# A hybrid attention and state-space block on one core: the last unit's sums of one head on VectorE, w_out split earlier, and the gates' loads and buffers

## The chip, the cores and the metric

The kernel runs on one core of a Trainium2 chip. Its engines work side by side, each through a queue of its own in the order of that queue: TensorE (PE in the profile, its weight loads PEld), VectorE (DVE), ScalarE (ACT), GpSimd (POOL) and SyncE (SP), which here only issues transfers. The metric is the device time of one execution in microseconds; lower is better.

## The reference

One layer of a hybrid encoder: a normalised input is projected once and feeds attention and a state-space layer, whose gated and normalised outputs are joined and projected.

```python
xn = rmsnorm(h, pre_norm_w)                       # h: 16 meta tokens + 2048 tokens, width 1024
proj = einsum('bld,de->ble', xn, w_in)
q_lat, kv_lat, k_rope, attn_gate, ssm_u, ssm_gate = split(proj, ...)
...                                               # q, k (64 + 32 rotary) and v for 8 heads
y_attn = block_attention(qf, kf, vf)              # softmax(q k / sqrt(96)) v, bidirectional
y_attn = rmsnorm(y_attn * silu(attn_gate), attn_out_norm_w)
...
y_ssm = s5(forward) + s5(backward) + ssm_d * ssm_u
y_ssm = glu(gelu(y_ssm))                          # w_glu, b_glu
y_ssm = rmsnorm(y_ssm * silu(ssm_gate), ssm_out_norm_w)
y = einsum('bld,de->ble', concat([y_attn, y_ssm]), w_out)
return (h + rmsnorm(y, post_norm_w))[:, 16:]
```

All is float32. The kernel gets the precision from three matmuls of rounded parts: high x high, high x low, low x high.

## The kernel before, in words

**A planner sets each engine's order.** The kernel's parts are Python generators (streams). A planner keeps a modelled clock for each engine, lets each stream name what it needs next (`Need`: data, an engine, PSUM banks, a condition), and issues the stream that could start first, then by rank. A stream with a due time waits behind the others until the attention's `progress` has reached it; `progress` is the number of the unit plus the share of it that is issued. So the order on each engine is fixed when the program is built. Every engine call goes through one helper, so all rows of the profile show line L190, and the names of the tiles tell them apart.

**Gates.** For 8 blocks of 256 tokens, `gates` multiplies the tokens (`x2h`, `x2l`, loaded by `gates_prep` from `xt_d` in four transfers a block) with the gates' weights, in 8 groups `m` of 48 matmuls `pg`. ACT copies each result into a buffer `gs`, of which there are three, and SP writes it to `gate_d`. Beside it runs the state-space layer: PE's `z` matmuls need `mbt`, an ACT copy, and `md` tables come in eight transfers a group on SP's queue.

**Attention.** 16 units (4 pairs of heads by 4 blocks of 512 queries). `b_main` takes 17 key tiles `t` by two heads `h`: three `sc` matmuls on PE, the exponential `pp` on ACT (12 buffers), and a sum over the key tiles, `acc[h]`, for the softmax's denominator, one add a tile from `t` = 1 on, on POOL. In the last unit, 15, the two adds of `t` = 15 and the two of `t` = 16 go to DVE. `b_pv` follows with the `pv` matmuls in groups of three or four tiles. After each unit, `finish` adds up `acc` over the partitions (`sm` on PE, a copy `sms` on ACT), takes reciprocals in four pieces on DVE, sends them through memory and scales the unit's output `ot` with it and with the gate `gt` on POOL.

**Preparation of the output projection.** `glu_main` ends with the split of w_out: 8 slices of 128 rows, two halves each, with two ACT operations (`ws_o` into a PSUM bank, the cast `wo`) and a subtraction on DVE (`wo`, `wo_l`) for each half; after the last, POOL scales the post-norm weights, `pw`. Only then the streams `c_stat` and `c_split` are added. `c_stat` squares a block of 256 tokens on ACT (`sq_c`), adds it up on DVE and over the partitions on PE (`pss`); `c_split` splits the tokens into high and low (`yy`, ACT and DVE). Block 0 needs only the attention's units up to 12.

**Tail.** `c_late` does the output projection, `po`, in 24 matmuls a segment of 512 columns, for 16 tiles of 128 tokens, and `c_post` the post-norm and the residual.

Of the kernel before, what the change touches and what calls it, by code (L numbers as in the profile page):

```python
# [11 lines left out]
F32 = mybir.dt.float32  # L12
# [3 lines left out]
ALU = mybir.AluOpType  # L16
# [4 lines left out]
P = 128  # L21
D = 1024
EPS = 1e-6
NJ = 16
# [243 lines left out]
def body(ctx: ExitStack, tc: tile.TileContext, x, meta_tokens, pre_norm_w, post_norm_w, w_in,  # L268
# [5 lines left out]
    V, A, PE, POOL, SP = (Engine(clock, n, e) for n, e in (  # L274
        ("V", nc.vector), ("A", nc.scalar), ("PE", nc.tensor), ("P", nc.gpsimd), ("SP", nc.sync)))
# [57 lines left out]
    pools, stacks, floors = {}, {}, {"left": 0.0, "right": 0.0}  # L333
# [8 lines left out]
    def close_pool(name):  # L342
        st, side = stacks.pop(name)
        st.close()
        pools.pop(name)
        floors[side] = max([clock.last(t) for t, h in clock.home.items() if h[0] == name] + [floors[side]])

    psum = Pool(clock, "psum", ctx.enter_context(tc.tile_pool(name="psum", bufs=1, space=PSUM)), 0.0)
    banks = {"a": (0, 1), "b": (2, 3), "c": (4, 5), "d": (6,), "e": (7,), "de": (6, 7),
             "sc": (0, 1, 5), "sc3": (0, 1, 5, 4), "pm": (2, 3, 6), "pm0": (6, 7, 1), "k0": (4, 5), "g": (2, 3, 0), "y": (7, 1), "gl": (4,)}  # L350
# [5 lines left out]
    def pst(use, name, shape=(P, 512)):  # L356

        k = next_bank(use)
        turns[use] += 1
        return psum.tile(shape, F32, tag=f"ps_{k}", name=name)  # L360
# [11 lines left out]
    done = {}  # L372
# [218 lines left out]
    def split(hi, lo, src, scale=None):  # L591

        if scale is None:
            A.copy(hi, src)
            V.tensor_tensor(lo, src, hi.bitcast(F32), ALU.subtract)
        else:
            A.activation(hi, src, AF.Copy, scale=scale)
            V.scalar_tensor_tensor(lo, src, scale, hi.bitcast(F32), ALU.mult, ALU.subtract)
# [14 lines left out]
    def pair(p):  # L613

        return ((slice(0, 2), (0, 1)), (slice(0, 3, 2), (1, 0)), (slice(1, 3), (0, 1)))[p % 3]
# [482 lines left out]
    def gates_prep():  # L1098
        xg = pools["xg"]
        st["rrow2"] = xg.tile([P, 2, P], F32, name="rrow2")  # L1100
        SP.dma_start(st["rrow2"].rearrange("p t c -> p (t c)"),
                     rx_d.rearrange("t c -> (t c)").unsqueeze(0).broadcast_to([P, 256]))
        gx[7] = tuple(x3[h].rearrange("p s k c -> p k s c")[:, :, pair(7)[0]] for h in "hl")
        for n, b in enumerate(GO):
            if n == 0:
                continue
            yield Need(when=lambda n=n: done.get("gate", 0) >= n - 1)
            xx = [(xg if n % 2 else xp).tile([P, 8, 2, P], F32R, tag="x" + h, name="x2" + h) for h in "hl"]
            for t in range(2):
                for x_ in range(2):  # L1110
                    SP.dma_start(xx[x_][:, :, t].bitcast(F32), xt_d[2 * b + t, x_])
            gx[b] = xx
            done["gx"] = n

    def gates():
        for b in GO:
            yield Need(when=lambda b=b: b in gx)
            xh, xl = gx.pop(b)
            for m in range(8):
                yield Need(banks=["g"])  # L1120
                pg = pst("g", "pg", (P, 2, P))
                for k in range(8):
                    if k % 2 == 0:
                        yield Need(when=lambda k=k: done.get("wg", 0) >= k + 2)
                        yield Need(st["wg_l"][k], st["wg_l"][k + 1], xl[:, k], xl[:, k + 1])
                    for i, (xx, ww) in enumerate(((xh, "wg_h"), (xh, "wg_l"), (xl, "wg_h"))):
                        PE.matmul(pg, st[ww][k][:, m * P:(m + 1) * P], xx[:, k],
                                  start=(k == 0 and i == 0), stop=(k == 7 and i == 2))
                gs = pools["xg"].tile([P, 2, P], F32, tag="gs", name="gs", bufs=3)
                if b == 0:  # L1130

                    yield Need(pg, st["rrow2"])
                    V.tensor_tensor(gs, pg, st["rrow2"], ALU.mult)
                elif b < 7:
                    A.copy(gs, pg)
                else:
                    for t_, t in enumerate(pair(7)[1]):
                        A.copy(gs[:, t], pg[:, t_])
                SP.dma_start(gate_d[m, :, b * 256:(b + 1) * 256], gs.rearrange("p t c -> p (t c)"))
            done["gate"] = done.get("gate", 0) + 1  # L1140
        close_pool("xg")
        close_pool("xp")
        close_pool("wt")
        order.add(b_open2(), -2)
# [326 lines left out]
    def b_open2():  # L1471

        yield Need(when=lambda: "kp" in pools)
        open_pool("bst", "right")
        open_pool("gl", "right")
        b_load_v(0)
        order.add(b_main(), 0)
        order.add(b_pv(), 0.2)
        order.add(b_gate(), -2.5)
        order.add(glu_main(), -0.5)  # L1480

    def b_load_v(p):
        vp = pools["bst"].tile([P, 17, P], F32, tag="vp", name="vp", bufs=2)
        SP.dma_start(vp[:, 0:NJ], v_d[0:NJ, :, p * P:(p + 1) * P].rearrange("j c e -> c j e"))
        SP.dma_start(vp[:16, NJ], v_d[NJ, :16, p * P:(p + 1) * P])
        vps[p] = vp
# [135 lines left out]
    def b_main():  # L1622
        bs = pools["bst"]
        for u in range(16):
            p, qb = divmod(u, 4)
            b = p % 2
            yield Need(when=lambda u=u: u in qts)
            if qb == 1 and p < 3:
                b_load_v(p + 1)
            qh, ql = qts.pop(u)  # L1630
            yield Need(when=lambda u=u: done.get("fin", 0) >= u - 1)
            acc = [bs.tile([P, 512], F32, tag=f"acc{h}", name=f"acc{h}", bufs=2) for h in range(2)]
            accs[u], first = acc, []
            for t in range(17):
                n = P if t < NJ else 16
                ks = slice(t * P, t * P + n)
                for h in range(2):

                    bk = "sc3" if "glu" in done else "sc"
                    yield Need(qh[h], banks=[bk],  # L1640
                               when=lambda k=(2 * (17 * u + t) + h - PPB) // 2: done.get("pv", 0) > k)
                    sc = pst(bk, "sc")
                    PE.matmul(sc[:n], kh[b, h][:, ks], qh[h], start=True, stop=False)
                    PE.matmul(sc[:n], kl[b, h][:, ks], qh[h][0:96], start=False, stop=False)
                    PE.matmul(sc[:n], kh[b, h][0:96, ks], ql[h], start=False, stop=True)
                    pp = bs.tile([P, 512], F32, tag="pp", name="pp", bufs=PPB)
                    A.activation(pp[:n], sc[:n], AF.Exp, scale=SCALE)
                    if t == 1:
                        POOL.tensor_tensor(acc[h], first[h], pp, ALU.add)
                    elif t > 1:  # L1650
                        (V if u == 15 and t >= NJ - 1 else POOL).tensor_tensor(acc[h][:n], acc[h][:n], pp[:n], ALU.add)
                    if t == 0:
                        first.append(pp)
                    pps.setdefault((u, t), []).append(pp)
                    order.progress = u + (t + 0.5 * h + 0.5) / 17
            done["unit"] = u + 1
            clock.lat = 2.2
# [28 lines left out]
    def glu_main():  # L1686
# [3 lines left out]
        for k in range(4):  # L1690
            raw = gl.tile([P, D], F32, tag="ysv", name="rawl", bufs=2)
# [8 lines left out]
        for b in range(8):  # L1700
# [30 lines left out]
            for m in range(4):  # L1731
                for half_ in range(2):
                    mm = m + 4 * half_
                    for k in range(4):
                        if k % 2 == 0:
                            yield Need(gl_, banks=["gl"] if (half_, k) == (0, 0) else [],
                                       due=d0 + (mm_ + 1) * 1.2 / 18)
# [21 lines left out]
        for k in range(8):  # L1759
            raw = pools["kp"].tile([P, D], F32, tag="k00" + "01"[k % 2], name="rawo")  # L1760
            SP.dma_start(raw, w_out[k * P:(k + 1) * P, :])
            if k == 7:

                yield Need(when=lambda: "q15" in done)
                st["wo"][1].append(pools["qp"].tile([P, D], F32R, tag="q4", name="wo_l7", bufs=1))
            for hv in range(2):
                c = slice(hv * 512, hv * 512 + 512)
                yield Need(raw, eng="A V", banks=["pm"], due=12.6 + k * 0.36 + hv * 0.18)
                ws = pst("pm", "ws_o")
                A.activation(ws, raw[:, c], AF.Copy, scale=cols[:, AOW + k:AOW + k + 1])  # L1770
                split(st["wo"][0][k][:, c], st["wo"][1][k][:, c], ws)
# [221 lines left out]
```

## Time and profile before

| what | us |
| --- | --- |
| median of 3 runs | 1697.39 (1694.19 to 1698.38) |
| profiled execution, its own time | 1692.8 |
| its span in the profile | 1691.0 |
| mean granted clock of PE in it | 0.99 of full speed |

The span is what the profiler saw from the first to the last instruction; the time of the same execution is 1.8 us more. Of the span, PE is busy nearly all, and the slices of the page in which it is not are few. The start times of rows count from the span's start: PE's last `pv` of unit 15 ends at about 1479, and the tail follows.

### The profile page before, as it was taken

What the parts mean: (1) busy time and instruction counts of PE and PEld (TensorE: products, weight loads), DVE (VectorE), ACT (ScalarE), POOL (GpSimd) and SP (SyncE); (2) the same over time, 40 slices, a digit from 0 to 9 for tenths busy, and PEclk for the clock granted to TensorE, in tenths of its full rate; (3) what the DMA queues carried; (4) which work ended last, traced back from release to release, by engine and by line L of the source; (5) the groups of instructions that cost most, each with busy time, mean ns of one, the idle gap of its engine ahead of it and who ended that gap; (6) DMA issues with size and microseconds to landing.
All of it is one profiled execution on the core that took longest, in us unless ns stands there. A gap on an engine that the chain in (4) does not pass through costs nothing. (4 is left out here: it accounts for less than half of the span.)

```text
span 1691.0 us, 28589 instructions
## 1 busy us (share of the span) xinstructions
PE 1641.0 (97%) x10320; PEld 1278.0 (76%) x10320; DVE 1082.2 (64%) x2543; ACT 781.4 (46%) x1628; POOL 805.8 (48%) x686
## 2 busy tenths in 40 slices
PE   8999999999989999999999999999999999979998
PEld 7897999999989966667767676767676666557776
DVE  5688634899987466665556557555745556157775
ACT  4543334435535246444444545354544555534433
POOL 0010012000000157877787778787878999922222
PEclk9999999999999999999999999999999999989999
DMA  9865645463445652112111202121111011123431
GB/s 221 267 209 145 208 141 174 125 176 117 143 135 166 157 151 86 41 57 66 42 59 40 75 25 63 54 70 36 45 41 59 27 60 58 64 92 138 150 125 50
DMA packets 179539, 175.68 MB, mean 104 GB/s; under 512 B 35419, under 2 KB 153110, under 8 KB 178118
## 3 DMA queue, kind: packets, MB, share of 16 engines
q1 hardware_dynamic: 179382, 173.86, 33.7%
q8 instruction: 81, 1.33, 0.3%
q14 instruction: 60, 0.49, 0.1%
q10 hardware_dynamic: 16, 0.00, 0.0%
HBM read 110.28 MB, written 63.54 MB: 103 GB/s over the span
## 5 line engine op out<-in xcount | busy, mean ns | idle before, releaser
L190 POOL TENSOR_TENSOR acc<-acc,pp 128x512 f32<-128x512 f32 (+1 forms) x476 | 595.2, 1283 | 87.4 <-ACT pp L190 86.9
L190 ACT ACTIVATE pp<-sc 128x512 f32<-128x512 f32 (+1 forms) x544 | 320.1, 598 | 319.5 <-PE sc L190 303.3
L190 DVE TENSOR_REDUCE mx<-pm 128x1 f32<-128x412 f32 (+1 forms) x640 | 340.3, 580 | 129.0 <-PE pm L190 126.8
L190 PE MATMUL sc<-qh,kh 97*128 97x512 f32 (+1 forms) x544 | 220.7, 406 | 1.8 <-DVE qh L190 1.8
L190 PE MATMUL sc<-qh,kl 96*128 96x512 f32 (+1 forms) x544 | 217.0, 399 | 0.0
L190 PE MATMUL sc<-ql,kh 96*128 96x512 f32 (+1 forms) x544 | 215.3, 396 | 0.0
L190 PE MATMUL pm<-kh,qh 96*128 96x412 f32 (+1 forms) x640 | 187.9, 359 | 0.6 <-ACT qh L190 0.2
L190 PE MATMUL po<-wo,yy 128*128 128x512 f32 (+1 forms) x759 | 181.5, 393 | 0.1
L190 PEld LDWEIGHTS po<-wo,yy 128*128 128x128 f32 x759 | 140.6, 190 | 34.4 <-ACT rps L190 1.2
L190 PEld LDWEIGHTS pm<-kh,qh 96*128 96x128 f32 x640 | 115.8, 188 | 55.2 <-issue 18.6
L190 PE MATMUL pg<-x2h,wg_h 128*128 128x256 f32 x448 | 130.4, 291 | 0.0
L190 PEld LDWEIGHTS sc<-qh,kh 97*128 97x128 f32 (+1 forms) x544 | 100.0, 184 | 38.5 <-issue 20.2
L190 PE MATMUL pg<-x2h,wg_l 128*128 128x256 f32 x448 | 126.7, 283 | 0.0
L190 PE MATMUL pg<-x2l,wg_h 128*128 128x256 f32 x448 | 126.6, 283 | 0.0
L190 PEld LDWEIGHTS sc<-ql,kh 96*128 96x128 f32 (+1 forms) x544 | 101.0, 186 | 27.2
L190 POOL TENSOR_TENSOR ta<-qs,cs 128x512 f32<-128x512 f32 x8 | 10.9, 1365 | 221.9 <-ACT qs L190 136.3
L190 POOL TENSOR_TENSOR t_c<-o_c,pw 128x512 f32<-128x512 f32 (+1 forms) x33 | 41.9, 1269 | 145.4 <-DVE o_c L190 124.6
L190 PEld LDWEIGHTS sc<-qh,kl 96*128 96x128 f32 (+1 forms) x544 | 101.1, 186 | 10.8
L190 POOL COPY U<-um 128x4 f32<-128x4 f32 x16 | 5.5, 349 | 214.9 <-issue 147.4
L190 PE MATMUL pa_c<-gh,wl 128*128 128x256 f32 x512 | 103.8, 284 | 0.6 <-DVE gl__13652 L190 0.6
L190 PEld LDWEIGHTS pa_c<-gh,wl 128*128 128x128 f32 x512 | 84.0, 190 | 6.3 <-issue 2.5
L190 PEld LDWEIGHTS pg<-x2h,wg_h 128*128 128x128 f32 x448 | 85.7, 191 | 1.4 <-issue 1.2
(458 smaller groups left out, 3344.8 us busy)
## 6 DMA issues: line engine op xcount, KB each, us to landing
raw<-in_x_dram SPq DMA_DIRECT2D x16, 512.0 KB
gate_d<-gs SPq DMA_DIRECT2D x64, 128.0 KB
md<-g_d SPq DMA_DIRECT2D x64, 128.0 KB
xt_c<-in_x_dram SPq DMA_DIRECT2D x8, 1024.0 KB
out_dram<-o_c SPq DMA_DIRECT2D x15, 512.0 KB
xt_d<-x3h SPq DMA_DIRECT2D x14, 512.0 KB
xt_d<-x3l SPq DMA_DIRECT2D x14, 512.0 KB
x2h<-xt_d SPq DMA_DIRECT2D x14, 512.0 KB
```

The costliest lines, as they stand in the source:

```text
L190: r = f(*args, **kw)
```

## The change

Four edits. The loads of a block's tokens for the gates, `x2h` and `x2l`, each wait until a given number of gate writes has been issued. `gs` gets a fourth place. In unit 15, head 1's sums go to DVE and all of head 0's stay on POOL. And the due times of the w_out split begin at 12.0 and follow more closely.

```diff
@@ gates_prep
             for t in range(2):
                 for x_ in range(2):
+                    yield Need(when=lambda n=n, t=t, x_=x_: done.get("gm", 0) >= 8 * (n - 1) + (0, 1, 3, 5)[2 * t + x_])
                     SP.dma_start(xx[x_][:, :, t].bitcast(F32), xt_d[2 * b + t, x_])
@@ gates
-                gs = pools["xg"].tile([P, 2, P], F32, tag="gs", name="gs", bufs=3)
+                gs = pools["xg"].tile([P, 2, P], F32, tag="gs", name="gs", bufs=4)
...
                 SP.dma_start(gate_d[m, :, b * 256:(b + 1) * 256], gs.rearrange("p t c -> p (t c)"))
+                done["gm"] = done.get("gm", 0) + 1
@@ b_main
                     if t == 1:
-                        POOL.tensor_tensor(acc[h], first[h], pp, ALU.add)
+                        (V if u == 15 and h else POOL).tensor_tensor(acc[h], first[h], pp, ALU.add)
                     elif t > 1:
-                        (V if u == 15 and t >= NJ - 1 else POOL).tensor_tensor(acc[h][:n], acc[h][:n], pp[:n], ALU.add)
+                        (V if u == 15 and h else POOL).tensor_tensor(acc[h][:n], acc[h][:n], pp[:n], ALU.add)
@@ glu_main
-                yield Need(raw, eng="A V", banks=["pm"], due=12.6 + k * 0.36 + hv * 0.18)
+                yield Need(raw, eng="A V", banks=["pm"], due=12.0 + k * 0.33 + hv * 0.16)
```

What the planner makes of it shows in the order of each engine. On SP, in the stretch of the gates in which PE waits longest, the queue before is this (`gate_d<-gs` is the write of a gate):

```order
L190 DMA x2h<-xt_d 128x8x128
L190 DMA gate_d<-gs 128x256
L190 DMA md<-g_d 128x1x256 x8
L190 DMA x2l<-xt_d 128x8x128
L190 DMA x2h<-xt_d 128x8x128
L190 DMA x2l<-xt_d 128x8x128
L190 DMA gate_d<-gs 128x256 x4
```

And with the change, the same stretch:

```order
L190 DMA x2h<-xt_d 128x8x128
L190 DMA gate_d<-gs 128x256
L190 DMA md<-g_d 128x1x256 x8
L190 DMA gate_d<-gs 128x256
L190 DMA x2l<-xt_d 128x8x128
L190 DMA x2h<-xt_d 128x8x128
L190 DMA gate_d<-gs 128x256
L190 DMA x2l<-xt_d 128x8x128
L190 DMA gate_d<-gs 128x256 x2
```

Two gate writes have moved ahead of loads; the `md` loads stay ahead of both. On DVE, from the last rows of the w_out split before the end of the attention on, the queue before (`acc_16067` and `acc_16068` are the two heads' sums of unit 15, `sms` the row sums, `yy` and `sq_c` block 0 of the tail):

```order
L190 TENSOR_TENSOR wo_l_16052<-ws_o,wo 128x512 x2
L190 SCALAR_TENSOR_TENSOR gt<-tg,gt 128x512
L190 TENSOR_TENSOR acc_16067<-acc_16067,pp 128x512
L190 TENSOR_TENSOR acc_16068<-acc_16068,pp 128x512
L190 TENSOR_TENSOR acc_16067<-acc_16067,pp 16x512
L190 TENSOR_TENSOR acc_16068<-acc_16068,pp 16x512
L190 RECIPROCAL sms<-sms 128x64 x4
L190 TENSOR_TENSOR yy<-yt,yy 128x1024 x2
L190 TENSOR_TENSOR sq_c<-sq_c 128x512
L190 TENSOR_TENSOR sq_c<-sq_c 128x256
```

And with the change, from the start of unit 15 (`acc_16081` is head 1's sum; the recips are unit 14's):

```order
L190 TENSOR_TENSOR acc_16081<-pp 128x512
L190 RECIPROCAL sms<-sms 128x64 x3
L190 TENSOR_TENSOR yy<-yt,yy 128x1024
L190 TENSOR_TENSOR acc_16081<-acc_16081,pp 128x512 x2
L190 TENSOR_TENSOR yy<-yt,yy 128x1024
L190 TENSOR_TENSOR acc_16081<-acc_16081,pp 128x512 x2
L190 RECIPROCAL sms<-sms 128x64
L190 TENSOR_TENSOR sq_c<-sq_c 128x512
L190 TENSOR_TENSOR sq_c<-sq_c 128x256
L190 TENSOR_TENSOR acc_16081<-acc_16081,pp 128x512 x2
L190 TENSOR_TENSOR sq_c<-sq_c 128x512
L190 TENSOR_TENSOR sq_c<-sq_c 128x256
```

The w_out split is over before this stretch, and block 0's `yy` and `sq_c` now stand among head 1's adds of unit 15 instead of behind its recips. On PE, the matmuls that wait for `sq_c` stand here before, behind the end of unit 15:

```order
L190 MATMUL pv__16105<-pp,vp 64x512 x8
L190 MATMUL sm<-acc_16067,ones 32x256 x2
L190 MATMUL sm<-acc_16068,ones 32x256 x2
L190 MATMUL pss<-sq_c,ones 32x128 x4
L190 MATMUL po_16445<-wo,yy 128x512 x12
```

And with the change, within unit 15; the `pv` group is that of the key tiles 3 to 5:

```order
L190 MATMUL pv__16118<-pp,vp 64x512 x6
L190 MATMUL sc<-qh_15665,kh 128x512
L190 MATMUL sc<-qh_15665,kl 128x512
L190 MATMUL sc<-ql_15666,kh 128x512
L190 MATMUL pss<-sq_c,ones 32x128 x4
L190 MATMUL sc<-qh_15669,kh 128x512
L190 MATMUL sc<-qh_15669,kl 128x512
L190 MATMUL sc<-ql_15670,kh 128x512
```

`pss` of block 0 has moved ahead of some two thirds of unit 15's matmuls, all of which stand behind it in PE's queue. POOL's `pw` product has moved with the split, from behind unit 15's last add to before the last four adds of unit 14.

## Rows read from the trace of the kernel before

**Rows 1.** The page: busy time of each engine, share of the span, instructions.

```profile
PE 1641.0 (97%) x10320; PEld 1278.0 (76%) x10320; DVE 1082.2 (64%) x2543; ACT 781.4 (46%) x1628; POOL 805.8 (48%) x686
```

**Rows 2.** By stretch: us, busy PE, PEld, DVE, ACT, POOL; granted clock; DMA share, GB/s.

```profile
490.00:500.00 10.00, 7.11 (x61) 6.78 (x62) 9.63 (x21) 0.86 (x2) 0.00 (x0) 0.83 0.15 47
1400.00:1450.00 50.00, 50.00 (x226) 29.71 (x224) 27.03 (x54) 29.25 (x53) 45.53 (x38) 1.00 0.19 64
1450.00:1500.00 50.00, 39.33 (x163) 21.73 (x162) 13.58 (x16) 18.30 (x29) 33.48 (x26) 0.86 0.31 105
```

**Rows 3.** PE's waits: total us, times, the longest.

```profile
PE pss L190 <- DVE sq_c L190: 9.9, 8, 5.8
PE z L190 <- ACT mbt L190: 5.9, 6, 4.7
```

**Rows 4.** Timeline of PE, gates: start, us, operation, [idle before <- releaser].

```profile
459.00 1.96 PE L190 MATMUL z<-U,mbt 128*64 128x128 f32 x30 [0.25 <-ACT mbt L190]
...
462.43 0.38 PE L190 MATMUL py<-xx,mc_re 128*128 128x128 f32 x2
...
492.89 3.08 PE L190 MATMUL z<-U,mbt 128*64 128x128 f32 x30 [4.68 <-ACT mbt L190]
...
497.90 0.38 PE L190 MATMUL py<-xx,mc_re 128*128 128x128 f32 x2
```

**Rows 5.** Timeline of ACT and of SP's queue, the same place.

```profile
475.58 0.38 ACT L190 COPY gs<-pg 128x256 f32<-128x256 f32 x1 [2.51 <-PE pg L190]
...
491.98 0.37 ACT L190 COPY gs<-pg 128x256 f32<-128x256 f32 x1 [4.29 <-DMA gate_d<-gs]
492.25 0.59 ACT L190 COPY mbt<-pt_mb 128x512 f32<-128x512 f32 x1
...
473.23 0.65 SPq L190 DMA_DIRECT2D gate_d<-gs  x1
...
485.60 7.10 SPq L190 DMA_DIRECT2D gate_d<-gs  x4
```

**Rows 6.** Timeline of PE, unit 15 and its end.

```profile
1457.26 0.50 PE L190 MATMUL sc<-qh,kh 97*128 97x512 f32 x1
...
1482.78 1.67 PE L190 MATMUL sm<-acc,ones 128*32 128x256 f32 x8 [3.61 <-DVE acc L190]
1490.27 0.64 PE L190 MATMUL pss<-sq_c,ones 128*32 128x128 f32 x4 [5.82 <-DVE sq_c L190]
...
1492.72 7.37 PE L190 MATMUL po<-wo,yy 128*128 128x512 f32 x22
...
1500.15 5.52 PE L190 MATMUL po<-wo,yy 128*128 128x512 f32 x23
```

**Rows 7.** Timeline of POOL and DVE, the same stretch.

```profile
1459.56 18.66 POOL L190 TENSOR_TENSOR acc<-acc,pp 128x512 f32<-128x512 f32 x15
1478.16 2.80 POOL L190 TENSOR_SCALAR pw<-pw 128x1024 f32<-128x1024 f32 x1
...
1477.02 2.75 DVE L190 TENSOR_TENSOR acc<-acc,pp 128x512 f32<-128x512 f32 x1 [16.83 <-POOL acc L190]
1479.69 0.68 DVE L190 TENSOR_TENSOR acc<-acc,pp 128x512 f32<-128x512 f32 x1
...
1484.90 1.79 DVE L190 RECIPROCAL sms<-sms 128x64 f32<-128x64 f32 x4 [1.57 <-ACT sms L190]
1487.94 1.22 DVE L190 TENSOR_TENSOR yy<-yt,yy 128x1024 fp32r<-128x1024 f32 x1
1489.08 1.15 DVE L190 TENSOR_TENSOR sq_c<-sq_c 128x512 f32<-128x512 f32 x2
```

**Rows 8.** Timelines: ACT's sums of unit 14; POOL and DVE in the tail.

```profile
1441.73 0.37 ACT L190 COPY sms<-sm 128x256 f32<-128x256 f32 x1
...
1510.18 1.29 POOL L190 TENSOR_TENSOR t_c<-o_c,pw 128x512 f32<-128x512 f32 x1 [1.44 <-DVE o_c L190]
...
1510.28 2.27 DVE L190 TENSOR_TENSOR yy<-yt,yy 128x1024 fp32r<-128x1024 f32 x1 [0.18 <-ACT yy L190]
```

## The prediction

> **What bounds the kernel now.** The page's table of busy time comes first: the matmul engine PE is busy 1641.0 of 1691.0 us, VectorE (DVE) 64%, GpSimd (POOL) 48%, ScalarE (ACT) 46% [rows 1]. Work taken from another engine is therefore worth only what it takes out of a hole of PE, or out of a stretch in which PE runs at the lower of its two clock levels. So the next view is busy time by stretch: from 1400 to 1450 PE is busy 50.00 of 50, from 1450 to 1500 only 39.33, at a mean granted clock of 0.86; from 490 to 500 it is 7.11 of 10 at 0.83 [rows 2]. The list of PE's waits then names what ends these holes: a copy `mbt` of ACT, 4.7 us at the longest, and the sum of squares `sq_c` on DVE, 5.8 at the longest [rows 3]. The change touches both places, and nothing else of it lies where PE waits today.
>
> **The gates, near 488 us.** In the timeline PE's `z` matmuls stop for 4.68 us before 492.89; one unit of this stage earlier the same wait is 0.25 [rows 4]. ACT tells why. Its copy of a gate at 491.98 waited for the landing of a `gate_d` write, and the `mbt` copy stands right behind it in ACT's queue. With three places for `gs` that copy takes the place filled at 475.58, three copies back. On SP's queue no `gate_d` write was issued between 473.23 and 485.60: eight `md` loads and three x2 loads, which the order of SP's queue names, stood in between [rows 5]. With four places the copy takes the one before, whose write left at 473.23, and with the loads spaced out one gate write is ahead of all three x2 loads and another ahead of the last of them. Either edit should end the wait.
> The price: stall 4.68 - 0.25 = 4.43. Behind the hole PE runs at the lower clock for a while: from the start of the 30 `z` to the first `py` it is 497.90 - 492.89 = 5.01, against 462.43 - 459.00 = 3.43 in the undisturbed unit [rows 4], so 1.58 more. Sum 4.43 + 1.58 = **6.0 saved**. The lower bound is 4.43 (PE has the same work and the clock comes down elsewhere), or 0 if another transfer takes the place of this one (a rival below). I cost the later start of the x2 loads at nothing: a block's tokens are loaded during the block before, and one block is more than the 33.9 us between the two `z` rows [rows 4], against a shift of some 10 us at most.
>
> **The end of unit 15.** Today PE ends the last `pv` at 1482.78 - 3.61 = 1479.17 and starts the first `po` at 1492.72, 13.55 us later; the 22 `po` that follow take 7.37, where the next 23 take 5.52, or 0.24 each, which makes 5.28 for 22: 2.09 more of lower clock [rows 6]. Together 15.64. What must stay is `sm` at full clock, 1.67 / 2 = 0.84, and the two `pss` at about 0.6: **14.2 can be won**. What fills the hole: 3.61 us for the sums (four last adds on DVE, the first of them 2.75 us instead of 0.68, and POOL's fifteen in a row from 1459.56 to 1478.22, late by then), then 5.82 for the recips, `yy` and `sq_c` of block 0, which DVE runs after the sums [rows 6, 7].
> The change empties it twice. Head 1's 16 adds leave POOL, so POOL needs 16 x 1.24 = 20 us for head 0's, where 32 took 40, and both heads' sums end with the exponentials. And because the w_out split and the `pw` product are done in unit 14, the planner puts block 0's statistics into unit 15: `yy` and `sq_c` between head 1's adds on DVE, `pss` between two `sc` groups on PE. So `sm` and `po` follow the last `pv` with next to no gap.
>
> **The new wait.** PE takes its queue in order, so `pss` in the middle of unit 15 holds all `sc` and `pv` behind it until DVE is through. DVE's queue up to the second `sq_c` pair begins when ACT has copied unit 14's row sums, 1441.73 + 0.37 = 1442.10. It holds four recips (1.79), two `yy` (2 x 1.2), six adds (6 x 0.68), two pairs of `sq_c` (2 x 1.15): 10.6 us, to 1452.7 [rows 7, 8]. PE reaches `pss` after the `pv` of tiles 3 to 5 and one more `sc` group; in the old trace the `sc` groups behind that `pv` begin at 1457.26 [rows 6]. In the new order the `pv` stands two `sc` groups earlier (six matmuls of 0.24, 1.4), and one group (0.7) stands between it and `pss`: 1457.26 - 1.4 + 0.7 = 1456.6. By this no wait at all.
> But a DVE operation with two inputs in SBUF seems to wait while POOL works: `yy` took 2.27 where it began at 1510.28, just after POOL's `t_c` at 1510.18, and 1.22 where POOL was idle [rows 7, 8]; it ended 1.08 after POOL's 1511.47, which is about its own time. The add at 1477.02 took 2.75 instead of 0.68 in the same way [rows 7]. Twelve of DVE's operations here have two inputs, and POOL is in an add most of that time, though less than today (its adds of the unit are halved); I take that two of three wait one POOL operation of 1.29: 8 x 1.29 = 10.3, so `sq_c` ends at 1463.0. PE then waits 1463.0 - 1456.6 = 6.4 and pays 1.6 of lower clock after it, as behind the hole of the gates: **8.0 lost**. Bounds: none of twelve waits (0 lost), or all twelve wait one operation, 15.5, so 1468.2 and 11.6 + 1.6 = 13.2 lost.
> The Trainium skill's page "SBUF — State Buffer", section "Who interferes with whom", says that a DVE instruction with two SBUF inputs contends with a GpSimd instruction that reads SBUF, and that whoever issues first holds the shared ports for the whole instruction. By that rule no operation waits longer than one of POOL's, so the time would lie between 1677 and 1690 and the slower rival below falls. The `yy` at 1510.28 agrees within 0.14 us; the add at 1477.02 waited 2.07, more than one POOL add of 1.24, and by that row the time would be the slower rival's 1700.
>
> **Costed at nothing.** The split of w_out begins half a unit earlier. Each half row is two ACT operations and one DVE subtraction, on engines that are busy 29.25 and 27.03 of 50 between 1400 and 1450, while PE has no idle time there [rows 2]. If three of them in a row push an exponential back, PE may lose up to 1 us a unit, 2 in all. `pw`, 2.80 on POOL [rows 7], now stands ahead of unit 14's last four adds; those sums are wanted only by `finish`, and if that is late the bound is 2.8.
>
> **Sum.** 6.0 + 14.2 - 8.0 = 12.2 saved. The profiled execution took 1692.8, so 1680.6 by it; it lies 4.6 below the median of the three runs, 1697.39, and I put the saving to that median: 1697.4 - 12.2 = **1685**.
>
> **The rivals.**
> No contention: the waits of `yy` have another cause, DVE ends at 1452.7, ahead of PE. Then 20.2 saved, 1677.2. For it: `yy` rows without POOL's company are short, and POOL has half its adds. Against: the rows above. Chance 0.20.
> Full contention: all twelve wait, 13.2 lost, 7.0 saved, 1690.4. For it: POOL's 15 adds without a gap [rows 7]. Against: it has fewer adds after the change. 0.15.
> The gates wait anyway, for another write or load on SP's queue: 6.2 saved, 1691.2. For it: `md` still stands ahead of the writes. Against: four places reach a write issued 15 us before it is wanted. 0.05.
> Slower: each of the twelve waits like the add at 1477.02, 2.07 us: 24.8, to 1477.5, and PE stands for 20.9 + 1.6 = 22.5 of lost time against 14.2 + 6.0 won: 1699.7. It decides from (14.2 + 6.0 - 1.6 + 3.9) / 12 = 1.9 us for each. Against: no row but one shows it, and a POOL operation is only 1.29. 0.08.
> The remaining 0.52 is the forecast, with a range of its own of 1681 to 1688 (6 to 10 operations that wait).
>
> **How the numbers follow.** A change of 0.3%, 5.1 us, is about what a measurement of this kernel can tell from none, so "no change" is 1692.3 to 1702.5. Forecast and the first two rivals lie below it, the third at its edge, the fourth inside. With something for the terms costed at nothing, faster 0.86, same 0.11, slower 0.03. The range from 1676 to 1692 holds the forecast and the first three rivals, and leaves out the fourth and some of the spread.
>
> **What would show it.** Right: in PE's list of waits no `mbt` wait above 1 us, and no `gs` copy that waits for a `gate_d` write; `sm` and `po` right behind the last `pv`; a wait of `pss` for `sq_c` of some 6 us in the middle of unit 15, near 1450 on the new clock; DVE adds there of 0.7 to 2.0 us. Wrong: a `pss` wait of none (first rival) or above 11 us; a new wait of `sc` for ACT's exponentials or of `sm` for unit 14's sums (the terms costed at nothing); a hole left at the end of unit 15 because a sum still ends late.

## The result, and the profile after

| | us | runs |
| --- | --- | --- |
| before | 1696.35 median (1694.19 to 1698.38) | 4 |
| changed | 1675.94 median (1674.11 to 1676.67) | 4 |
| ratio | 0.9878, 95% interval 0.9861 to 0.9895 | |

The change saves 20.4 us of the median, 17.8 to 23.6 by the interval; a second set of runs of the same kernel, further below, gives 17.3. The forecast was a saving of 12.2 and a time of 1685, in a range of 1676 to 1692: the first median lies just under that range, the second, 1678.96, in it. The profiled execution of the changed kernel took 1676.39, its span is 1674.6.

The busy times of the engines over the span, beside [rows 1]:

```profile
PE 1639.6 (98%) x10320; PEld 1279.5 (76%) x10320; DVE 1091.7 (65%) x2555; ACT 780.7 (47%) x1628; POOL 798.7 (48%) x674
```

PE has the same work; what went is mostly its idle time, 50.0 us before (1691.0 - 1641.0) and 35.0 now (1674.6 - 1639.6). By stretch, beside [rows 2], with the gates' hole on the new clock:

```profile
480.00:490.00 10.00, 9.79 (x99) 9.21 (x100) 9.68 (x23) 9.76 (x27) 0.00 (x0) 1.00 0.72 202
...
1450.00:1500.00 50.00, 44.57 (x194) 27.20 (x191) 28.44 (x39) 22.21 (x37) 23.40 (x16) 0.90 0.29 101
```

The hole of the gates is closed at full clock; from 1450 to 1500 PE still lacks 5.4 us, at a granted clock of 0.90.

The list of PE's waits follows. In the changed kernel its first rows and that of `mbt` are these (total us, times, the longest):

```profile
PE pss L190 <- DVE sq_c L190: 4.5, 1, 4.5
PE pv L190 <- ACT lt L190: 2.6, 1, 2.6
...
PE z L190 <- ACT mbt L190: 1.3, 6, 0.2
...
PE sc L190 <- ACT pp L190: 1.0, 1, 1.0
```

Beside [rows 3], the long `mbt` wait is gone, and of eight `pss` waits one is left. Two are new in kind: this one `pss` wait lies inside unit 15, and once `sc` waits for an exponential.

The gates, PE and ACT, to be held against [rows 4, 5] (start, us, operation, what ended the idle time before it):

```profile
460.48 1.96 PE L190 MATMUL z<-U,mbt 128*64 128x128 f32 x30 [0.23 <-ACT mbt L190]
...
489.90 1.96 PE L190 MATMUL z<-U,mbt 128*64 128x128 f32 x30 [0.21 <-ACT mbt L190]
493.33 0.38 PE L190 MATMUL py<-xx,mc_re 128*128 128x128 f32 x2
...
489.02 0.35 ACT L190 COPY gs<-pg 128x256 f32<-128x256 f32 x1
489.27 0.58 ACT L190 COPY mbt<-pt_mb 128x512 f32<-128x512 f32 x1
```

From one `z` row to the next it is 29.42 us, before 33.89, and from the second to the first `py` 3.43, before 5.01: 4.47 + 1.58 = 6.05. The copy of a gate waits for no write any more.

Unit 15 and its end on PE, beside [rows 6]; the first row is the row sums of unit 14, from which unit 15 is counted here. In the kernel before that row stands at 1441.03.

```profile
1436.01 0.64 PE L190 MATMUL sm<-acc,ones 128*32 128x256 f32 x8
...
1451.86 0.50 PE L190 MATMUL sc<-qh,kh 97*128 97x512 f32 x1 [0.96 <-ACT pp L190]
1452.75 0.41 PE L190 MATMUL pss<-sq_c,ones 128*32 128x128 f32 x4
1457.63 0.64 PE L190 MATMUL pss<-sq_c,ones 128*32 128x128 f32 x4 [4.46 <-DVE sq_c L190]
...
1479.88 3.80 PE L190 MATMUL pv__16118<-pp,vp 128*64 128x512 f32 x16
1483.61 0.64 PE L190 MATMUL sm<-acc,ones 128*32 128x256 f32 x8
1484.18 5.40 PE L190 MATMUL po<-wo,yy 128*128 128x512 f32 x22
```

`sm` and `po` follow the last `pv` without a gap, and 22 `po` take 5.40 instead of 7.37. But from row sums to row sums unit 15 takes 1483.61 - 1436.01 = 47.60, where it took 41.75 with the wait for the sums in it.

DVE in the same stretch, beside [rows 7, 8]:

```profile
1437.12 1.38 DVE L190 RECIPROCAL sms<-sms 128x64 f32<-128x64 f32 x3 [2.08 <-ACT sms L190]
1439.50 1.56 DVE L190 TENSOR_TENSOR yy<-yt,yy 128x1024 fp32r<-128x1024 f32 x1 [1.00 <-ACT yy L190]
1440.98 3.46 DVE L190 TENSOR_TENSOR acc<-acc,pp 128x512 f32<-128x512 f32 x2
1444.37 2.29 DVE L190 TENSOR_TENSOR yy<-yt,yy 128x1024 fp32r<-128x1024 f32 x1
1446.59 2.58 DVE L190 TENSOR_TENSOR acc<-acc,pp 128x512 f32<-128x512 f32 x2
...
1449.54 1.08 DVE L190 TENSOR_TENSOR sq_c<-sq_c 128x512 f32<-128x512 f32 x2
1452.32 3.12 DVE L190 TENSOR_TENSOR acc<-acc,pp 128x512 f32<-128x512 f32 x2 [1.70 <-ACT pp L190]
1455.37 2.20 DVE L190 TENSOR_TENSOR sq_c<-sq_c 128x512 f32<-128x512 f32 x2
```

Two adds take 3.46, not 1.4, and the second pair of `sq_c` 2.20, not 1.1. The queue runs from 1437.12 to 1457.57, 20.5 us.

The tail, from the first `po` to the last, as one window of each kernel, before and then changed (columns as in rows 2):

```profile
1492.70:1683.90 191.20, 188.22 (x850) 148.49 (x848) 126.77 (x245) 75.36 (x149) 42.46 (x33) 0.99 0.31 110
```

```profile
1484.20:1667.50 183.30, 183.30 (x852) 146.15 (x848) 118.84 (x239) 73.97 (x149) 46.17 (x34) 1.00 0.33 119
```

The tail is 7.9 us shorter, of which the first 22 `po` explain 2.0. This the prediction does not have.

All in one table, worked from the `z`, `py`, `sm` and `po` rows of each trace. The gates' unit is from the `z` at three quarters of all `z` matmuls to the `py` at three quarters; unit 15 from row sums to row sums; the end from these to the first `po` (negative where `po` stands ahead of `sm`); the tail to the last `po`.

| kernel | gates' unit | unit 15 | end | tail | last three |
| --- | --- | --- | --- | --- | --- |
| before | 44.2 | 41.8 | 9.9 | 191.2 | 242.9 |
| changed | 38.2 | 47.6 | 0.6 | 183.3 | 231.5 |
| changed, second measurement (after_again) | 38.2 | 47.9 | 0.6 | 183.3 | 231.8 |
| only the fourth place (g_four) | 38.2 | 41.8 | 9.9 | 192.5 | 244.2 |
| only the spaced loads (g_space) | 38.2 | 41.7 | 9.9 | 191.9 | 243.6 |
| tail's order put back (a_lag) | 38.2 | 47.3 | 0.6 | 186.6 | 234.5 |
| head 0's adds left out (noadd0) | 38.2 | 38.7 | 0.6 | 183.3 | 222.6 |
| pss later (late_pss) | 38.2 | 40.4 | 0.6 | 183.3 | 224.3 |
| pss and a square later (late_both) | 38.2 | 38.6 | 0.6 | 183.3 | 222.5 |
| both heads on DVE (u15_dve) | 38.2 | 38.6 | 0.6 | 184.5 | 223.7 |
| statistics behind unit 15 (a_stat_end) | 38.2 | 38.1 | 8.9 | 191.2 | 238.2 |
| only the due times (e_due) | 44.9 | 43.7 | -3.0 | 186.1 | 226.8 |
| only the sums (e_sums) | 46.4 | 42.0 | 0.6 | 183.3 | 225.9 |
| changed without the sums (a_nosums) | 38.2 | 43.6 | -3.0 | 186.1 | 226.7 |
| tail's order given to before (b_lead) | 44.6 | 41.7 | 9.9 | 188.6 | 240.3 |

### The profile page after: what moved, and what is told of

It reads as the page before. It is cut to its first block, busy times and chain, and to the rows that moved or that the text cites. A ratio compares the mean times of both kernels' runs of the same rounds, so it can differ in the third digit from the quotient of the medians.

```text
span 1674.6 us, 28574 instructions
## 1 busy us (share of the span) xinstructions
PE 1639.6 (98%) x10320; PEld 1279.5 (76%) x10320; DVE 1091.7 (65%) x2555; ACT 780.7 (47%) x1628; POOL 798.7 (48%) x674
## 4 chain that ended last, share of the span: by engine, by line
PE 79%; DVE 10%; ACT 4%; DMA 4%; issue 2%; SPq 1%; POOL 0%; DVEq 0%; ACTq 0%; POOLq 0%
PE sc L190 23%; PE po L190 11%; PE pm L190 7%; PE pa_c L190 6%; PE pg L190 5%; PE pu L190 3%; PE pa L190 3%; PE py L190 2%; DVE s0t L190 1%; PE pq L190 1%; PE pv__12516 L190 1%; PE pv__10317 L190 1%; PE pv__11421 L190 1%; PE pv__14228 L190 1%; PE pv__10832 L190 1%
## 5 line engine op out<-in xcount | busy, mean ns | idle before, releaser
L190 POOL TENSOR_TENSOR acc<-acc,pp 128x512 f32<-128x512 f32 (+1 forms) x465 | 584.4, 1290 | 103.9 <-ACT pp L190 102.8
L190 POOL TENSOR_TENSOR t_c<-o_c,pw 128x512 f32<-128x512 f32 (+1 forms) x33 | 43.6, 1321 | 137.4 <-DVE o_c L190 107.8
```

Source lines behind the costliest of these rows:

```text
L190: r = f(*args, **kw)
```

## The experiments

**Which edit ends the gates' wait.** Each of the two edits by itself, on the kernel before. The fourth place:

```diff
-                gs = pools["xg"].tile([P, 2, P], F32, tag="gs", name="gs", bufs=3)
+                gs = pools["xg"].tile([P, 2, P], F32, tag="gs", name="gs", bufs=4)
```

> The kernel before with only the fourth place for gs; the loads are not spaced out. If one more place is enough by itself, the 4.7 us wait of z for the mbt copy near 488 us goes, PE passes the end of the gates' stage about 6.1 us earlier on its trace than before, and nothing changes behind it: about 1690 us. If the spacing of the loads is what did it, the wait stays (0 saved, about 1696). If half of it came from each, about 3 us.

And the spaced loads (with the counter `done["gm"]` of the change):

```diff
+                    yield Need(when=lambda n=n, t=t, x_=x_: done.get("gm", 0) >= 8 * (n - 1) + (0, 1, 3, 5)[2 * t + x_])
                     SP.dma_start(xx[x_][:, :, t].bitcast(F32), xt_d[2 * b + t, x_])
```

> The kernel before with only the loads of the gates' tokens spaced out; gs keeps three places. Theory: the gate write is issued right behind the md loads, some 3.6 us earlier, and lands about when the copy wants its place: 5 to 6 us saved, about 1690 us, with an mbt wait of at most 1 us. Rival (the place decides, since the write still stands behind eight md loads): the wait stays at 3 us or more, about 1693 to 1696.

One run each: 1689.37 and 1689.99 us, beside a median before of 1693.61; single runs say little, and the argument rests on the traces. In both the gates' unit takes 38.2 instead of 44.2, and the longest `mbt` wait is 0.3 and 0.2. Either edit is enough, and the second adds nothing to the first: the place that the copy takes is free in time if it is another place, and also if the write of the same place leaves before the loads. The rivals fall. (The tails of these two kernels, 1.3 and 0.7 us longer in the table, hold a wait of `po` for `o_c` of 1.1 and 1.2; neither edit touches the tail.)

**Whether the tail's order is worth the rest.** In the kernel before, an `o_c` and the `yy` of the next tile stand on DVE between the two `sq_c` pairs of a block; in the changed kernel the pairs stand side by side, and PE's `pss` stands one segment of 24 `po` earlier. The changed kernel with that part of the order put back:

```diff
             for t in range(2):
+                if b and t:
+                    yield Need(when=lambda b=b: done.get("cs", 0) >= 2 * b + 1)
                 yield Need(yt, eng="A")
```

> The changed kernel, but in the tail the second half of each block's statistics (from block 1 on) is held back until the next tile's yy has been issued, which is the order that the kernel before has there; unit 15 and its end are as in the changed kernel. Theory (5.9 us of the gain lie in the tail, where the kernel before lets pss wait for sq_c once a block and the changed kernel does not): six pss waits of 0.4 to 0.6 us come back and the tail from the first to the last po takes 188 to 190 us instead of 183.3: about 1681 us. Rival (the tail is faster for another reason, the clock after the hole for instance): 183 to 184 us, and 1676.

It took 1680.29 us (ratio to before 0.9917, 0.9902 to 0.9932), and the tail 186.6. So 3.3 of the 5.9 came back, less than the 188 to 190 expected, and the listed `pss` waits of the later blocks did not. The direction is the theory's, the size is not: the `yy` between the pairs is only a part of the order. `pss` of the later blocks stands 18 `po` later here than in the changed kernel, and 24 later in the kernel before.

The next kernel holds block 0's statistics until unit 15 has been issued, so that the planner makes the old tail by itself:

```diff
-            yield Need(when=lambda b=b: done.get("fin", 0) >= 12 + b // 2 + 1 and done.get("cs", 0) >= 2 * b - 2)
+            yield Need(when=lambda b=b: done.get("unit", 0) == 16 and done.get("fin", 0) >= 12 + b // 2 + 1 and done.get("cs", 0) >= 2 * b - 2)
```

> The changed kernel with block 0's statistics held until unit 15 is issued, as they stand in the kernel before; the sums stay on DVE. Theory: unit 15 loses its pss wait (38 to 39 us, -9), but between the last pv and the first po lie 9 to 10 us again (recips, yy and sq_c behind sm, +9, and 2 of lower clock), and the tail has the order of the kernel before and takes 187 to 189 us instead of 183.3 (+4 to +6, beside the clock): 1680 to 1684 us. Rival (the tail's gain has nothing to do with where block 0's statistics stand): tail 183 to 185 us with the clock, 1677 us.

1683.53 us (0.9929, 0.9915 to 0.9944). The tail is back at 191.2, all 7.9 of it, the first `po` at the lower clock included, and the end at 8.9; unit 15 falls to 38.1. The order of the tail hangs on where block 0's statistics stand, and with it the whole term.

The last test gives the order to the kernel before. The counter `done["pss"]` is set behind the `pss` matmuls:

```diff
-            yield Need(y, eng="A", when=lambda j=j: done.get("out", 0) >= j - 1)
+            yield Need(y, eng="A", when=lambda j=j: done.get("out", 0) >= j - 1 and (j < 2 or done.get("pss", 0) > j // 2))
```

> The kernel before with one rule more in the tail: the yy of tile 2b, from b = 1 on, waits in the plan until block b's pss has been issued, so that both sq_c pairs stand side by side on DVE and pss stands, from block 3 on, where the changed kernel has it. Gates, sums, w_out split, unit 15 and its end are as before. Theory (the tail's share of the gain comes from this order alone, about 1 us a block): the tail from the first po to the last takes 185 to 187 us instead of 191.2, with the listed pss waits of 0.4 to 0.6 us gone in most blocks: 1690 to 1692 us. Rival (the tail gains from something that the stretch ahead of it leaves behind, for instance that block 0 is done earlier): 190 to 192 us in the tail, no gain.

1690.95 us (0.9975, 0.9964 to 0.9985), and a tail of 188.6, between what the two theories say. The `pss` rows of PE tell why. From block to block in the middle of the tail, before, then in the changed kernel, in this one, and in the one with a part of the order put back:

```profile
1606.48 0.41 PE L190 MATMUL pss<-sq_c,ones 128*32 128x128 f32 x4
1607.45 0.41 PE L190 MATMUL pss<-sq_c,ones 128*32 128x128 f32 x4 [0.56 <-DVE sq_c L190]
1607.79 5.42 PE L190 MATMUL po<-wo,yy 128*128 128x512 f32 x22
...
1630.39 0.41 PE L190 MATMUL pss<-sq_c,ones 128*32 128x128 f32 x4
```

```profile
1587.35 0.42 PE L190 MATMUL pss<-sq_c,ones 128*32 128x128 f32 x8
1587.70 5.41 PE L190 MATMUL po<-wo,yy 128*128 128x512 f32 x22
...
1610.29 0.43 PE L190 MATMUL pss<-sq_c,ones 128*32 128x128 f32 x8
```

```profile
1578.35 0.43 PE L190 MATMUL pss<-sq_c,ones 128*32 128x128 f32 x8
...
1601.30 0.42 PE L190 MATMUL pss<-sq_c,ones 128*32 128x128 f32 x8
```

```profile
1571.09 0.76 PE L190 MATMUL pss<-sq_c,ones 128*32 128x128 f32 x8
...
1594.38 0.77 PE L190 MATMUL pss<-sq_c,ones 128*32 128x128 f32 x8
```

A block takes 23.91 before, 22.94 in the changed kernel, 22.95 with the order alone and 23.29 with a part of it put back. The price shows from the first `pss` to the `po` behind it: 1607.79 - 1606.48 = 1.31 before, 1587.70 - 1587.35 = 0.35 in the changed kernel, so 0.96 a block. So the order alone is worth that once the tail is under way. The six blocks with a listed wait lose 0.76 to 0.96 each in the kernel before, 5.3 of the 5.9 us. In the kernel with the order given to it the first blocks lose a part again: `pss` waits 1.1 and 0.6 in blocks 1 and 2, and one `po` 0.8 for `o_c`. That this comes from block 0 not being ahead there fits, but no run shows it by itself.

**Whether DVE waits for POOL.** The changed kernel without fifteen of the sixteen adds of head 0 in unit 15; that head's row sums then lack those tiles. DVE's order is the same row for row, and PE's too in unit 15.

```diff
-                    elif t > 1:
+                    elif t > 1 and (u < 15 or h):
```

> The changed kernel without fifteen of head 0's sixteen adds on POOL in unit 15 (the row sums of that head are then wrong by what is left out); PE's and DVE's orders are the same row for row. Theory (DVE's operations with two inputs in SBUF wait for POOL's): DVE's adds of unit 15 take 0.7 us each instead of 0.7 to 2, the queue up to the second sq_c pair ends some 6 us earlier, and pss waits less than 1 us instead of 4.5; unit 15 is 7 to 9 us shorter: about 1668 us. Rival (the adds are slow for a reason of DVE's own, or by waits for ACT): durations and the pss wait as in the changed kernel, 1676 us.

1669.36 us (0.9857, 0.9836 to 0.9878). No `pss` wait, unit 15 in 38.7. The same rows on DVE:

```profile
1438.06 1.38 DVE L190 RECIPROCAL sms<-sms 128x64 f32<-128x64 f32 x3 [1.88 <-ACT sms L190]
1440.43 1.23 DVE L190 TENSOR_TENSOR yy<-yt,yy 128x1024 fp32r<-128x1024 f32 x1 [1.00 <-ACT yy L190]
1441.58 1.49 DVE L190 TENSOR_TENSOR acc<-acc,pp 128x512 f32<-128x512 f32 x2
1443.33 1.23 DVE L190 TENSOR_TENSOR yy<-yt,yy 128x1024 fp32r<-128x1024 f32 x1 [0.27 <-ACT yy L190]
1444.47 1.48 DVE L190 TENSOR_TENSOR acc<-acc,pp 128x512 f32<-128x512 f32 x2
...
1446.33 1.09 DVE L190 TENSOR_TENSOR sq_c<-sq_c 128x512 f32<-128x512 f32 x2
1449.12 0.69 DVE L190 TENSOR_TENSOR acc<-acc,pp 128x512 f32<-128x512 f32 x1 [1.70 <-ACT pp L190]
1450.09 0.69 DVE L190 TENSOR_TENSOR acc<-acc,pp 128x512 f32<-128x512 f32 x1 [0.28 <-ACT pp L190]
1450.70 1.14 DVE L190 TENSOR_TENSOR sq_c<-sq_c 128x512 f32<-128x512 f32 x2
```

With POOL nearly idle the queue takes 1451.84 - 1438.06 = 13.8 us instead of 20.5. The contention is shown, and its price in this stretch is 6.7. The twelve operations with two inputs take 16.3 us in the changed kernel and 9.0 here, 7.2 more; the rest of the difference is that DVE waits a little longer for ACT here. One by one in the two traces, eight of the twelve are longer, by 0.3 to 1.1 us, and four are not.

The other way to take POOL out leaves nothing out: both heads' sums of unit 15 on DVE (the first add, of `t` = 1, alike).

```diff
-                        (V if u == 15 and h else POOL).tensor_tensor(acc[h][:n], acc[h][:n], pp[:n], ALU.add)
+                        (V if u == 15 else POOL).tensor_tensor(acc[h][:n], acc[h][:n], pp[:n], ALU.add)
```

> The changed kernel with both heads' sums of unit 15 on DVE, none on POOL; the planner then puts pss at 15.74. Theory (DVE waits for POOL, not for itself): DVE's adds take 0.7 us each although it has twice as many, sq_c is in time for pss, and sm follows the last pv at once: unit 15 of 39 to 41 us, 1668 to 1671 us. Rival (DVE's adds are slow by themselves, 1 to 1.7 us each as in the changed kernel): 32 adds and the statistics take 45 to 60 us, PE waits for pss or sm, and the time is 1680 us or more.

1668.20 us (0.9838, 0.9823 to 0.9852). By line and shape, DVE's adds of 512 columns from 1430 to 1476, in the changed kernel, then in this one (count, busy us, mean ns of one, idle before them):

```profile
L190 DVE TENSOR_TENSOR acc<-acc,pp 128x512 f32<-128x512 f32 x13 | 16.5, 1272 | 10.9 <-ACT pp L190 10.4
```

```profile
L190 DVE TENSOR_TENSOR acc<-acc,pp 128x512 f32<-128x512 f32 x28 | 19.3, 724 | 9.1 <-ACT pp L190 9.0
```

So 28 adds take 19.3 us where 13 took 16.5, as each takes 0.72 and not 1.27: POOL has no adds of this unit beside them.

**Whether the pss wait costs what unit 15 is longer by.** The changed kernel with `pss` of block 0 later in PE's queue:

```diff
+            if b == 0:
+                yield Need(when=lambda: order.progress > 15.7)
             yield Need(s2, banks=["d"])
```

> The changed kernel with block 0's pss held back until progress 15.7, so that it stands a fifth of a unit later in PE's queue; DVE's order up to the second sq_c pair is the same. Theory (the pss wait of 4.5 us and the low clock behind it are what unit 15 is longer by): PE comes to pss some 8 us later, after DVE's pair, and waits for nothing; unit 15 takes 39 to 41 us from sum to sum instead of 47.6, and the time is 1668 to 1670 us, 6 to 8 less than the changed kernel. Rival (DVE is the bound of the unit, and the wait only moves to sm): a wait of sm for acc of 4 us or more, 1676 us.

1671.90 us median (0.9863, 0.9847 to 0.9880), its profiled execution 1667.7. Unit 15 takes 40.4, as expected; the median is 2 us above the 1670 expected. The `pss` wait falls to 0.6, not to nothing, and the `sc` wait of 1.0 for an exponential stays, as that one stands in ACT's queue behind a square that waits for DVE. In the changed kernel that square is this row; the exponentials follow it at 1451.23:

```profile
1450.26 1.06 ACT L190 ACTIVATE sq_c<-yt 128x1024 f32<-128x1024 f32 x1 [6.43 <-DVE sq_c L190]
```

The next kernel holds that square back too, until progress 15.5, and `pss` until 15.75:

```diff
+                if t and not b:
+                    yield Need(when=lambda: order.progress > 15.5)
                 yield Need(yt, eng="A")
```

> The changed kernel with block 0's pss held back until progress 15.75 and the second of its squares on ACT until 15.5, so that no exponential stands behind a square that waits for DVE. Theory: the sc wait of 1.0 us for pp and the pss wait of 0.6 us that the later pss alone still has both go: 1666 to 1669 us. Rival (one of them returns elsewhere, as a wait of sm or of the tail's first pss): 1669 to 1672 us.

1668.42 us (0.9835, 0.9820 to 0.9850), unit 15 in 38.6, and PE without a gap for the 50 us from the row sums of unit 14 on:

```profile
1438.50:1488.50 50.00, 50.00 (x230) 29.56 (x229) 34.95 (x45) 28.81 (x47) 30.16 (x20) 1.00 0.32 104
```

Its interval and that of the kernel with both heads on DVE lie below those of the changed kernel, without touching. The wait goes by order alone, or by taking POOL out of the unit.

**What the due times and the sums do alone.** Each on the kernel before, as in the change's diff:

> The kernel before with only the earlier due times of the w_out split. The planner then puts block 0's statistics into unit 15 (pss at 15.35) and the tail in the changed kernel's order; the sums stay on POOL. Theory: no gain at the gates; DVE's queue to the second sq_c pair has no adds in it (6.5 us of work, up to 14 with POOL's operations), PE is at pss some 6 us earlier than in the changed kernel, waits 0 to 4 us; the sums end late, sm waits 3 to 4 us; the tail gains 5.9: 1680 to 1685 us, so most of the gain without the sums. Rival (the gain at the end of unit 15 needs the sums on DVE): 1690 us or more.

> The kernel before with only head 1's sums of unit 15 on DVE. The planner puts block 0's pss at 15.88 of the units, late enough for DVE, and the tail into the changed kernel's order. Theory: the gates keep their wait; unit 15 of 39 to 41 us with no pss wait above 1 us, sm and po right behind the last pv, tail of 184 to 186 us: 1676 to 1680 us. Rival (without the earlier w_out split the statistics come too late for the first po): a hole of 5 us or more ahead of po, 1684 us or more.

Only the due times: 1681.03 us (0.9909, 0.9891 to 0.9927). Only the sums: 1677.36 us (0.9893, 0.9873 to 0.9912). Each by itself brings block 0's statistics into unit 15 and the tail into the new order, and each takes 16 to 17 us out of the last three columns of the table. They do not add: together they take 11.4. The times came as expected. With the due times alone `pss` waits 1.8 us and `sm` 1.4, where 3 to 4 were expected for `sm`. With the sums alone `pss` stands so late in unit 15 that it waits for nothing, but `sc` waits 1.7 us for an exponential, so that the unit takes 42.0 and not 39 to 41.

The last pair is the changed kernel once more, and the changed kernel without the move of the sums:

> The changed kernel once more, beside the three others of this call, so that differences of 0.3% can be read on one chip: 1674 to 1677 us.

> The changed kernel without the move of head 1's sums: POOL has both heads' sums and DVE the last four, as before; the three other edits stay. Theory (the sums on DVE bring no gain beside the other edits, since they lengthen DVE's queue ahead of pss): from the traces of the kernel with the due times alone, the stretch from unit 14's row sums to the end takes 226.8 us against 231.5 in the changed kernel: 1670 to 1672 us, 4 to 6 less than the changed kernel. Rival (the sums on DVE are worth the 3.6 us for which sm waited): 1678 to 1681 us.

The changed kernel: 1678.96 us (0.9892, 0.9874 to 0.9909), 17.3 less than before, 3 us above its first measurement and above the 1677 expected. Its trace is 3.5 us behind the first one's at unit 14's row sums, 1439.49 against 1436.01, and only 0.3 us slower after that. Such differences arise early: the first `pg` matmul starts at 264.18 in one and at 265.80 in the other, and anywhere from 262.5 to 266.6 in the fifteen traces. So one stretch of two traces compares kernels more sharply than their times do.

Without the sums on DVE: 1670.98 us (0.9849, 0.9834 to 0.9864), faster by 8.0 in the medians and by 5.1 in the last three columns of the table. So the move of head 1's sums costs time beside the three other edits: it lengthens DVE's queue ahead of `pss`, while the late sums cost 1.4 us without it:

```profile
1444.96 0.41 PE L190 MATMUL pss<-sq_c,ones 128*32 128x128 f32 x4 [1.79 <-DVE sq_c L190]
1477.29 1.23 PE L190 MATMUL sm<-acc,ones 128*32 128x256 f32 x8 [1.36 <-DVE acc L190]
```

## Why the prediction was wrong, step by step

**The gates**: 6.0 forecast, 6.05 in the trace, and either edit by itself does it, as was said. Right.

**The end of unit 15**: 14.2 to be won. From the last `pv` to the first `po` it is 0.50 instead of 13.55, and the first 22 `po` are 1.97 faster: 15.0, of which half a microsecond of `pss` has moved into the unit. Right in the mechanism, and 0.8 short.

**The new wait**: 8.0 forecast. Against the 38.1 us of a unit 15 without `pss`, the changed kernel's 47.6 are 9.5. The place, the queue and its end are as described: 20.9 us of queue were forecast and 20.5 came. But that is in part luck, as two errors cancel: eight of twelve operations were held up by POOL, as forecast, but by 0.9 us on average and not 1.29, so POOL costs 6.7 to 7.2 and not 10.3; and DVE stands 1.0 and 1.7 us for ACT's cast and exponential, which the sum did not have. And the price behind the wait was too low: PE's two idle times make 5.4, and without them, in the kernel with POOL nearly idle, the unit is 8.9 shorter. So 3.5 stand beside the listed idle time, and not 1.6. Some 3 of them are the lower clock; from 1458 to 1464 it is granted at 0.50, and the `sc` matmuls there start 0.43 us apart and not 0.23:

```profile
1458.00:1464.00 6.00, 6.00 (x18) 4.56 (x15) 1.58 (x3) 2.01 (x4) 2.03 (x2) 0.50 0.07 25
```

The rest is the first pair of `pss`, 0.41 us that count as busy but that no longer run together with the second pair.

**Costed at nothing**: w_out and `pw`. The traces run level with each other through units 12 to 14 (the row sums are 5.0 us early in units 12, 13 and 14 alike). Right. The prediction named a new wait of `sc` for an exponential as a sign that these terms cost something. Such a wait came, 0.96 us, but from another cause, the square of block 0 in ACT's queue: it is gone in the kernel that holds that square back, where the w_out split and `pw` stand as in the changed kernel.

**What failed** is a sentence at the start: "The change touches both places, and nothing else of it lies where PE waits today." The row of `pss` that it rests on says 9.9 us in eight waits, the longest 5.8 [rows 3]. Only 5.8 and 1.2 of that lie at the end of unit 15. The other six waits stand in the tail, one a block, and in the planned order of the changed kernel `pss` of every later block stands at least one segment earlier too. The tail was left out of the sum: 5.9 us beside the clock, of which the waits listed are 2.9.

With it the sum is 6.05 + 15.0 - 9.5 + 5.9 = 17.5. The second measurement gives 17.3. The first gives 20.4, with an interval of 17.8 to 23.6 that the sum misses by 0.3; the 3 us between two measurements of one kernel are the early differences described above, as far as the traces show. From the 1697.4 that the forecast started from, 17.5 would have given 1679.9. The two profiled executions differ by 16.4 in span, as the changed one ran 1.5 us late at `z` (460.48 and 459.00), and 1.6 at the first `pg`, ahead of what the edits reach.

**The rivals**: of that without contention only the time, 1677.2, comes near; its mechanism is refuted by the run with POOL nearly idle. "Full contention" did not happen, as four of the twelve were not held up; nor did the slower one, as none was held up by more than 1.1 us; nor the gates' rival. Why the one add at 1477.02 in the kernel before took 2.07 more [rows 7], no run here shows.

## What to carry to other kernels

Read the count beside the total in a list of waits: where the longest wait is not all of it, find the others, and ask of a change in order what it does to each, since a pipeline that repeats keeps a shift for all its rounds. When an operation is moved into a busy stretch of an engine that works in order, put it behind the point at which its input is ready: the same statistics in the same unit cost 9 us or nothing. And try the edits of a change one by one; here two of four were the same cure twice, and two others each worked best without the other.

## What the hardware showed that was not expected

A small DVE operation can stand behind a whole run of POOL operations. In the changed kernel without the sums on DVE, the scaling of `vvc`, 128 x 2 elements, took 15.32 us; in the changed kernel the first of these took 1.23. DVE, then POOL in that stretch:

```profile
1458.97 15.32 DVE L190 TENSOR_SCALAR vvc<-vvc 128x2 f32<-128x2 f32 x1 [2.21 <-DMA vvc<-rs_d]
```

```profile
1459.39 14.88 POOL L190 TENSOR_TENSOR acc<-acc,pp 128x512 f32<-128x512 f32 x12
```

It ended at 1474.29, with the last of twelve POOL adds that follow each other without a gap, until 1474.27. In the kernel with the due times alone it happened again: this operation and the small one behind it took 14.98 us from 1466.77 on, beside twelve POOL adds of 14.91 from 1466.74 on. The adds with two inputs, where they meet POOL's, get their turn after one operation: in the changed kernel two DVE adds take 3.46 from 1440.98 on, and three POOL adds 4.98 over the same time, where three take 3.7 alone by [rows 7]:

```profile
1440.60 4.98 POOL L190 TENSOR_TENSOR acc<-acc,pp 128x512 f32<-128x512 f32 x3 [0.62 <-ACT pp L190]
```

The prediction drew on the Trainium skill, page "SBUF — State Buffer", section "Who interferes with whom", for the statement that the side which issues first holds the shared ports for the whole instruction; by that reading one POOL operation was the most that a DVE operation waits. The row of `vvc` does not agree: it waited through twelve. It has one input, where the prediction's reading was on operations with two; the twelve operations of that kind in unit 15 do agree, each held up by 1.1 us at most. Why the one form waits so long and the other doesn't, no run here shows.

And a wait in the middle of PE's queue costs more than the list says: in the tail 0.56 us of listed wait go with 0.96 us of time a block, in unit 15 5.4 of idle time with 8.9. In the tail this is not the clock, which is granted in full from 1605 to 1615 in the kernel before. The two pairs of `pss` take 0.42 together when they stand side by side, and 0.41 each when the second has to wait, so the first pair is time lost that the list counts as busy. In unit 15 it is that and, for the most part, the lower clock behind the wait.
